# A two-layer fp32 trunk on one core: radix sums, cosine products, weights' low parts and gates from GpSimd to VectorE, and the second MLP's last folds spread

## The chip, the core and the metric

One core of a Trainium2 chip runs the whole program in one launch. The metric is the device time in microseconds (us), the median over several executions. PE is TensorE (matrix products), DVE is VectorE, ACT is ScalarE, POOL is GpSimd, SP is the engine whose queue issues most DMAs. All data are 32-bit floats.

## The reference

The program is a two-layer backbone over 1024 latent tokens and 256 context tokens of width 1024. Each layer has one input projection whose columns are split among differential attention (with an axial rope on q and k), a short gated convolution and a two-dimensional Fourier mix, then an output projection, a gated residual with a layer norm, and a squared-ReLU MLP with another gated residual and layer norm. Cut to what matters here:

```python
px = modulate(x, sh1, sc1) @ w_in[l]                  # input projection
qx, kx, vx, ux, gbx, gcx, fx = split_proj(px)
qx = axial_rope(qx, rows, cols)                       # x*cos + shuffled(x)*sin
kx = axial_rope(kx, rows, cols)
fourier_mix(fx)                                       # real part of an FFT over tokens and channels
...
x = layer_norm(ALPHA * x + g1 * mix_x, ln1_g[l], ln1_b[l])
x = layer_norm(ALPHA * x + g2 * squared_relu_mlp(modulate(x, sh2, sc2), w_up[l], w_down[l]),
               ln2_g[l], ln2_b[l])
```

## The kernel before

**Products.** Every fp32 product is made of three matmuls over high and low parts (`mm3`, L233 to L235): high by high, high by low, low by high. The high part is a rounding cast, mostly on ACT; the low part is `lo` (L229), one subtraction x - high. So each operand must pass through a cast and a subtraction before PE can use it, and the third matmul of a group is the first that needs the stationary operand's low part.

**Order.** The parts of the program that the change touches run under a manual schedule: every engine gets its instructions in the order in which the code is written, and runs them first in, first out. Generators interleave the work of the units by hand.

**The input projection** (`in_steps`) walks over 15 units per layer (two heads each of q and k pairs, v, u, c, g). A unit of layer 0 is 1280 columns wide and contracts over 1024, so it is 24 matmuls for each piece of 512, 512 and 256 columns. While a unit runs, `slot` advances four kinds of side work: `weights()` (L808 to L812), which converts the next unit's weights with `wconv` (ACT cast L2290, low part L229); `qk` (L556 on), the rope of the last q or k: drain on ACT (L561 or L563), shuffle on DVE (L566), cosine product (L567), sine product (L568), sum (L570), split (L581, L229) and store; `fourier1` (L638 on), the token transform's first radix step, some sixteen sums and differences (L645 to L664) of tiles of 128, 256 and 512 columns for each half of f, then a cast (L669) and a low part; and `fourier_mats` (L722 and L755 are its casts), small matmuls between the units. For layer 0, `PW` puts the low parts of the weights for units 4 to 12 on POOL; the others are on DVE. The first pass of the modulation (L336, L338, products with L383) for later stages is spread among the same slots on DVE.

**The first MLP's end** (`finish_steps`) handles ten tiles of 128 tokens. For each tile PE makes two halves of 24 matmuls in all, DVE adds each half to the running sum (L2378), POOL multiplies it by the gate (`gate`, L2382), DVE adds the residual (L2386), then come bn_stats (L2392), small statistics (L1265 to L1269 on DVE, L1270 and L1271 on POOL) and the norm on ACT (L2394). In `turn` the normed tiles are transposed (L2417) and modulated (L2426, L2429) for the next layer's input projection.

**The second MLP's end** (`finish_last`, with `fold`, `hl` and `rload` in the function before it) has eight tiles. During the last products, a table `tail` says after which product what is done: `hl` loads and splits the last rows of the hidden activations, `fold(t)` multiplies the running sum of tile t by the gate (L2171, POOL) and adds the residual (L2172, DVE). In `finish_last` the call `pre(t)` folds four tiles more; then, per tile, two halves are added on DVE (L2335), with bn_stats (L2336), statistics, norm (L2316, ACT), the product with the norm's weight (L2318, POOL), the sum with its bias (L2321, DVE) and the store. The last tile ends with L2346 and L2348 on DVE.

Of the kernel before, what the change touches and what calls it, by code (L numbers as in the profile page):

```python
# [13 lines left out]
ALU = mybir.AluOpType  # L14
# [5 lines left out]
SEQ = 1024  # L20
# [15 lines left out]
BKU = {1: 2, 2: 1, 3: 2, 4: 2, 5: 1, 6: 1, 7: 2}  # L36
ORDER = ["q0 k1 k2* q1* v0 u0 c0 g0 u1 c1 g1 q2 k3 q3 v1", "k0 q0 k1* q1* v0 u0 c0 g0 u1 c1 g1 k2 q2 k3 q3 v1"]
BGK = 2
PW = ((3, 13), (20, 0))
FME = 0  # L40
BGF = 2
FMD = 2
# [103 lines left out]
class Prog:  # L146
# [255 lines left out]
    def fold(self, l, which, lc, ch, vecs):  # L402
        nc = self.nc
        A = self.sm([128, 2, KT], bufs=4, tag="fold")
        B = self.sm([128, 2, KT], bufs=4, tag="fold")
        for v in vecs:
            nc.vector.tensor_tensor(A[:, v], self.lnc[:, lc, which], self.modc[:, l, ch + 1, v], op=ALU.mult)
            nc.vector.tensor_tensor(B[:, v], self.lnc[:, lc, which + 1], self.modc[:, l, ch + 1, v], op=ALU.mult)
            nc.vector.tensor_tensor(B[:, v], B[:, v], self.modc[:, l, ch, v], op=ALU.add)
        return A, B  # L410
# [145 lines left out]
    def qk(self, ps, n, h, key):  # L556
        nc = self.nc
        x = self.s5()
        for s, o in ps:
            if key == "q":  # L560
                nc.scalar.mul(x[:, s], o, SCALE)  # L561
            else:
                nc.scalar.copy(x[:, s], o)  # L563
        yield
        sh = self.s4()
        nc.vector.stream_shuffle(sh, x[:, :SEQ], [i ^ 16 for i in range(32)])  # L566
        nc.gpsimd.tensor_tensor(x[:, :SEQ], x[:, :SEQ], self.rc, op=ALU.mult)  # L567
        nc.vector.tensor_tensor(sh, sh, self.rs, op=ALU.mult)  # L568
        yield
        nc.vector.tensor_tensor(x[:, :SEQ], x[:, :SEQ], sh, op=ALU.add)  # L570
        yield from self.split_out(x, n)
        hi, lo = self.hl_out.pop(0)
        dh = self.dr([128, TOK])
        dl = self.dr([128, TOK])
        self.store(dh[:, :n], hi[:, :n])
        self.store(dl[:, :n], lo[:, :n])
        self.qkd[(key, h)] = (dh, dl)
# [59 lines left out]
    def fourier1(self, f, n):  # L637
        nc = self.nc  # L638
        nr = n // 128
        eo = self.s4(F32, [128, 2, 4, 128])  # L640
        e, o = eo[:, 0], eo[:, 1]
        fv = f.rearrange("p (a q) -> p a q", q=128)
        R = self.s5(F32, [128, 10, 128])
        g = nc.gpsimd
        g.tensor_tensor(e, fv[:, 0:4], fv[:, 4:8], op=ALU.add)  # L645
        g.tensor_tensor(o, fv[:, 0:4], fv[:, 4:8], op=ALU.subtract)
        t = self.s4(F32, [128, 4, 128])
        g.tensor_tensor(t[:, 0:2], e[:, 0:2], e[:, 2:4], op=ALU.add)
        g.tensor_tensor(R[:, 0], t[:, 0], t[:, 1], op=ALU.add)
        g.tensor_tensor(R[:, 1], t[:, 0], t[:, 1], op=ALU.subtract)  # L650
        g.tensor_tensor(R[:, 3], e[:, 0], e[:, 2], op=ALU.subtract)
        g.tensor_tensor(R[:, 6], e[:, 1], e[:, 3], op=ALU.subtract)
        yield
        g.tensor_tensor(t[:, 2], o[:, 1], o[:, 3], op=ALU.subtract)
        g.tensor_tensor(t[:, 3], o[:, 1], o[:, 3], op=ALU.add)
        g.tensor_scalar(t[:, 2:4], t[:, 2:4], math.sqrt(0.5), 0.0, op0=ALU.mult, op1=ALU.add)
        g.tensor_tensor(R[:, 2], o[:, 0], t[:, 2], op=ALU.add)
        g.tensor_tensor(R[:, 4], o[:, 0], t[:, 2], op=ALU.subtract)
        yield
        g.tensor_tensor(R[:, 5], o[:, 2], t[:, 3], op=ALU.add)  # L660
        g.tensor_tensor(R[:, 7], o[:, 2], t[:, 3], op=ALU.subtract)
        if n > SEQ:
            g.tensor_tensor(R[:, 8], fv[:, 8], fv[:, 9], op=ALU.add)
            g.tensor_tensor(R[:, 9], fv[:, 8], fv[:, 9], op=ALU.subtract)  # L664
        yield
        yield
        hi = self.s5(F32R, [128, 10, 128])
        lo = self.s5(F32R, [128, 10, 128])
        nc.scalar.copy(hi[:, :nr], R[:, :nr])  # L669
        yield  # L670
        self.lo(lo[:, :nr], R[:, :nr], hi[:, :nr])
        self.comps.append((hi, lo))
# [109 lines left out]
    def in_steps(self, X, l, PS):  # L782
        nc = self.nc
# [13 lines left out]
        nxt = [0]  # L797
# [9 lines left out]
        def weights():  # L807
            need = 2 if units[min(nxt[0], len(units) - 1)][0] == "v" else 1  # L808
            if self.wraw and len(self.wrdy) < need:
                self.wconv(nc.gpsimd if PW[l][0] < nxt[0] < PW[l][1] else None)  # L810
            if len(self.wraw) < 1:
                self.wload()  # L812

        def slot(k):
            for g in list(post):
                if next(g, 0) == 0:
                    post.remove(g)
            weights()
            if not fq:
                tail()  # L820
                for _ in range(k if nxt[0] > BGF else 1):
                    next(bg, None)
# [36 lines left out]
        for i, u in enumerate(units):  # L859
# [21 lines left out]
            if u[0] in "kq":  # L881
                g = self.qk([(slice(0, m), ps[:, :m])], m, b, u[0])
            elif u[0] == "u":
                z[b] = self.s5()
                nc.scalar.copy(z[b][:, :n], ps[:, :n])
                g = None
            elif u[0] == "c":
                g = self.conv_gc(ps, l, b, n, z.pop(b))
            else:
                g = self.conv_gb(ps, b, n)  # L890
# [1156 lines left out]
    def down_blocks(self, l, NG):  # L2047
        nc = self.nc
        n = SEQ if l else TOK
        T, HB, NB = n // 128, n // 2, D // 2  # L2050
        act, v, g = nc.scalar, nc.vector, nc.gpsimd
# [105 lines left out]
        bk = {"x": [self.p1() for _ in al], "y": [self.p1() for _ in range(8 - TH)]}  # L2157
        W, H, S, HR = [], [], [], []
        xr = {}
        self.acc = acc  # L2160
        gate = lambda t: self.gs[int(t >= 8)][:, :D]

        def rload(t):
            if t < T:
                xr[t] = self.s5()
                self.load(xr[t][:, :D], self.X2d[t])

        def fold(t):
            if t < T:
                y = acc[t]  # L2170
                g.tensor_tensor(y, y, gate(t), op=ALU.mult)  # L2171
                v.scalar_tensor_tensor(y, xr.pop(t)[:, :D], ALPHA, y, op0=ALU.mult, op1=ALU.add)  # L2172
                rload(t + 2)

# [43 lines left out]
        P = lambda fn, *a: (lambda: fn(*a))  # L2218
        if l:
            tail = [[gload], [P(wl, 0)], [P(wl, 1), wm], [P(wl, 2), wm], [P(wl, 3), wm],  # L2220
                    [wm, P(rload, 0), P(rload, 1)], [P(hl, 0), P(hl, 1)], [P(fold, 0), P(hl, 2), P(fold, 1)],
                    [P(hl, 3), P(fold, 2), P(fold, 3)]]
            tail = {N - 4 * (9 - a) + b: f for a, fs in enumerate(tail) for b, f in enumerate(fs)}
        else:
            tail = {-20: P(wl, 0), -18: P(wl, 1), -16: whi, -15: wlo, -14: P(wl, 2), -13: whi, -12: wlo,
                    -11: P(hraw, 0), -10: whi, -9: wlo, -8: hconv, -7: P(hraw, 1), -6: P(wl, 3), -5: hconv,
                    -4: [P(hraw, 2), P(hraw, 3)], -3: [gload, P(rload, 0)], -2: hconv, -1: whi}
            tail = {N + k: f for k, f in tail.items()}
# [36 lines left out]
        evac(0)  # L2265
        if l:
            self.lastW = W
            self.finish_last(l, H, lambda: None, bk["x"] + bk["y"], lambda t: fold(t + 4))
            yield
            return  # L2270
        wlo()
# [83 lines left out]
    def finish_steps(self, l):  # L2355
        nc = self.nc
        T = TOK // 128
        A, B = self.fold(l + 1, 2, l, 0, (0, 1))
        W, H = self.lastW, self.lastH
# [19 lines left out]

        def gate(t):  # L2380
            y = self.acc[t]
            nc.gpsimd.tensor_tensor(y, y, self.gs[int(t >= 8)], op=ALU.mult)  # L2382

        def resid(t):
            y = self.acc[t]
# [13 lines left out]
        def down(t):  # L2399
            if t < T:  # L2400
                half(t, 0)
            if t:
                resid(t - 1)
            if t < T:
                half(t, 512)
            if t:
                norm(t - 1)
            if t < T:
                gate(t)
                rload(t + 1)  # L2410
# [109 lines left out]
```

## Time and profile before

| | |
|---|---|
| time, median of 3 runs | 2889.89 us (2889.15 to 2890.15) |
| profiled execution's own time | 2883.89 us |
| its span in the trace | 2882.0 us |
| mean granted PE clock over the span | 0.979 |
| PE busy | 2714.8 us (94%), 14290 matmuls |
| DVE busy | 1990.0 us (69%), 2921 instructions |
| ACT busy | 1157.7 us (40%), 1614 instructions |
| POOL busy | 1092.1 us (38%), 660 instructions |

A number is read as follows. The span runs from the first to the last event of one execution; its own time is 1.9 us more. A row of a timeline gives start, duration, engine, source line and tiles, and in square brackets how long the engine sat idle before it and what released it. A row of groups gives a line's count, summed time, mean in ns, and idle time. Durations of neighbours on one engine overlap a little, so starts tell the pace.

### The profile page before, as it was taken

What the parts mean: (1) busy time and instruction counts of PE and PEld (TensorE: products, weight loads), DVE (VectorE), ACT (ScalarE), POOL (GpSimd) and SP (SyncE); (2) the same over time, 40 slices, a digit from 0 to 9 for tenths busy, and PEclk for the clock granted to TensorE, in tenths of its full rate; (3) what the DMA queues carried; (4) which work ended last, traced back from release to release, by engine and by line L of the source; (5) the groups of instructions that cost most, each with busy time, mean ns of one, the idle gap of its engine ahead of it and who ended that gap; (6) DMA issues with size and microseconds to landing.
All of it is one profiled execution on the core that took longest, in us unless ns stands there. A gap on an engine that the chain in (4) does not pass through costs nothing.

```text
span 2882.0 us, 37823 instructions
## 1 busy us (share of the span) xinstructions
PE 2714.8 (94%) x14290; PEld 2325.7 (81%) x14290; DVE 1990.0 (69%) x2921; ACT 1157.7 (40%) x1614; POOL 1092.1 (38%) x660
## 2 busy tenths in 40 slices
PE   7899999999999999899998999999999999999986
PEld 5788888778899999788886788888778778778865
DVE  6658767844578886677775555677645777668887
ACT  4221156623444444533332421266624545454331
POOL 2511145733110000276656600155763000078795
PEclk9999999999999999999999999999999999999998
DMA  7234553347546553634343244653356465554451
GB/s 269 86 144 155 168 144 89 120 139 254 217 176 221 184 191 137 236 129 152 135 163 122 90 161 155 200 123 90 121 187 211 158 234 198 179 204 159 153 185 59
DMA packets 228746, 468.17 MB, mean 162 GB/s; under 512 B 18926, under 2 KB 116692, under 8 KB 228564
## 3 DMA queue, kind: packets, MB, share of 16 engines
q1 hardware_dynamic: 208392, 394.39, 41.9%
q10 hardware_dynamic: 17292, 61.93, 5.6%
q0 software_dynamic: 2880, 9.44, 0.9%
q8 instruction: 113, 1.85, 0.3%
q14 instruction: 69, 0.57, 0.1%
HBM read 322.36 MB, written 143.31 MB: 162 GB/s over the span
## 4 chain that ended last, share of the span: by engine, by line
PE 51%; DVE 7%; POOL 4%; issue 4%; DMA 4%; ACT 3%; SPq 0%; ACTq 0%; DVEq 0%; POOLq 0%
PE q L233 13%; PE q L235 13%; PE q L234 13%; PE p L233 2%; PE p L235 2%; PE p L234 2%; PE q L1020 2%; POOL a L229 1%; PE p L955 1%; PE p L956 1%; DVE a L229 1%; PE q L1007 1%; DMA a<-d 1%; DMA b<-wu 1%; POOL b L2382 1%
## 5 line engine op out<-in xcount | busy, mean ns | idle before, releaser
L233 PE MATMUL q<-a,a 128*128 128x512 f32 (+1 forms) x1611 | 586.8, 364 | 34.2 <-DVE b L2237 15.2
L235 PE MATMUL q<-a,a 128*128 128x512 f32 (+2 forms) x1658 | 599.3, 361 | 5.0 <-DVE a L229 5.0
L234 PE MATMUL q<-a,a 128*128 128x512 f32 (+1 forms) x1594 | 580.2, 364 | 3.4 <-POOL a L229 3.4
L234 PE MATMUL p<-a,b 128*128 128x512 f32 (+1 forms) x1064 | 397.1, 373 | 1.1 <-POOL a L229 1.0
L233 PEld LDWEIGHTS q<-a,a 128*128 128x128 f32 x1611 | 304.2, 189 | 82.5 <-ACT a L2098 10.9
L229 POOL TENSOR_TENSOR a<-b,a 128x256 fp32r<-128x256 f32 (+1 forms) x137 | 220.7, 1618 | 349.9 <-ACT a L2098 196.5
L235 PEld LDWEIGHTS q<-a,a 128*128 128x128 f32 x1658 | 313.1, 189 | 47.7 <-DVE a L229 6.1
L2237 DVE TENSOR_TENSOR b<-q,b 128x512 f32<-128x512 f32 x405 | 268.4, 684 | 108.4 <-PE q L235 107.3
L234 PEld LDWEIGHTS q<-a,a 128*128 128x128 f32 x1594 | 301.4, 189 | 45.8 <-POOL a L229 4.5
L229 DVE TENSOR_TENSOR a<-a,a 128x1024 fp32r<-128x1024 f32 (+4 forms) x163 | 271.1, 1665 | 41.8 <-ACT a L2095 21.4
L233 PE MATMUL p<-a,b 128*128 128x512 f32 (+1 forms) x792 | 295.1, 373 | 1.5 <-ACT b L2290 1.0
L235 PE MATMUL p<-a,b 128*128 128x512 f32 (+1 forms) x776 | 283.3, 365 | 4.0 <-POOL b L229 2.4
L233 PE MATMUL q<-b,a 128*128 128x256 f32 (+1 forms) x748 | 256.0, 342 | 14.9 <-DVE b L2378 6.0
L234 PE MATMUL q<-b,a 128*128 128x256 f32 (+1 forms) x748 | 253.4, 339 | 0.7 <-DVE b L229 0.7
L235 PE MATMUL q<-b,a 128*128 128x256 f32 (+1 forms) x748 | 253.0, 338 | 0.0
L338 DVE SCALAR_TENSOR_TENSOR m<-w,k,m 128x256 f32<-128x256 f32 x448 | 219.6, 505 | 20.6 <-DMA w<-wmr 11.0
L234 PEld LDWEIGHTS p<-a,b 128*128 128x128 f32 x1064 | 202.8, 191 | 32.7 <-POOL a L229 1.9
L965 DVE TENSOR_REDUCE c<-p 128x1 f32<-128x1280 f32 x128 | 190.7, 1490 | 55.5 <-PE p L956 42.1
L981 ACT ACTIVATE a<-p,c 128x1280 f32<-128x1280 f32 x128 | 170.4, 1331 | 68.6 <-DVE c L965 50.1
L233 PEld LDWEIGHTS q<-b,a 128*128 128x128 f32 x748 | 144.0, 192 | 37.5 <-DVE b L2378 7.3
L233 PEld LDWEIGHTS p<-a,b 128*128 128x128 f32 x792 | 150.8, 190 | 25.6 <-issue 2.7
L235 PEld LDWEIGHTS p<-a,b 128*128 128x128 f32 x776 | 147.4, 190 | 29.4 <-POOL b L229 3.3
(297 smaller groups left out, 5398.5 us busy)
## 6 DMA issues: line engine op xcount, KB each, us to landing
a<-d SPq DMA_DIRECT2D x85, 512.0 KB
w<-wmr SPq DMA_DIRECT2D x160, 256.0 KB
a<-d SPq DMA_DIRECT2D x56, 640.0 KB
b<-wu SPq DMA_DIRECT2D x64, 512.0 KB
d<-t SPq DMA_DIRECT2D x46, 640.0 KB
b<-wd SPq DMA_DIRECT2D x52, 512.0 KB
d<-a ACTq DMA_DIRECT2D x40, 640.0 KB
a<-d SPq DMA_DIRECT2D x80, 320.0 KB
```

The source lines that it names most:

```text
L229: (eng or self.nc.vector).tensor_tensor(out, x, hi, op=ALU.subtract)
L233: mm(out, lh, rh, start=start, stop=False, skip_group_check=on)
L234: mm(out, lh, rl, start=False, stop=False, skip_group_check=on)
L235: mm(out, ll, rh, start=False, stop=stop, skip_group_check=on)
L338: nc.vector.scalar_tensor_tensor(a, w[:, i], s, a, op0=ALU.mult, op1=ALU.add)
L955: nc.tensor.matmul(ps[:, c:c + w], Q[p][:, qs], K[p][0][:, ks], start=True, stop=False)
L956: nc.tensor.matmul(ps[:, c:c + w], Q[p][:, qs], K[p][1][:, ks], start=False, stop=True)
L965: nc.vector.reduce_max(mx, ps[:, :nkey], axis=AX.X, negate=True)
L981: self.nc.scalar.activation(e[:, :nkey], ps[:, :nkey], AF.Exp, bias=mx, accum_out=s)
L1007: nc.tensor.transpose(pt[:, i], e, self.ident)
L1020: nc.tensor.matmul(po[:, :256], V[i // 8][:, i % 8], aT[i // 4][:, i % 4], start=i == 0, stop=i == 9)
L2237: v.tensor_tensor(a, ps, a, op=ALU.add)
```

## The change

Five edits. The cosine product of `qk` goes from POOL to DVE (16 instructions of 128x1024). The radix sums of `fourier1` go from POOL to DVE (four calls). `PW` is gone, so the low parts of the weights for units 4 to 12 of layer 0 are DVE's (10 of 128x1024). The gates of both MLPs' ends go from POOL to DVE (10 in `finish_steps`, 8 in `fold`). And the folds of the second MLP's end stand elsewhere: the table runs fold 0, `hl(2)`, fold 1, `hl(3)` after four products in turn, then fold 2; the other five folds are called from `finish_last` before tiles 0, 1, 2, 3 and 5 rather than before tiles 0 to 3 alone. What stays on POOL: the low parts of attention's and `turn`'s tiles, the gated weights `wm` (L2182), L2318, and the statistics L1270 and L1271. PE's order of instructions does not change.

```diff
-PW = ((3, 13), (20, 0))
@@ qk
-        nc.gpsimd.tensor_tensor(x[:, :SEQ], x[:, :SEQ], self.rc, op=ALU.mult)
+        nc.vector.tensor_tensor(x[:, :SEQ], x[:, :SEQ], self.rc, op=ALU.mult)
@@ fourier1
-        g = nc.gpsimd
+        g = nc.vector
@@ in_steps, weights()
-                self.wconv(nc.gpsimd if PW[l][0] < nxt[0] < PW[l][1] else None)
+                self.wconv()
@@ fold
-                g.tensor_tensor(y, y, gate(t), op=ALU.mult)
+                v.tensor_tensor(y, y, gate(t), op=ALU.mult)
@@ tail of the second MLP (l = 1)
-                    [wm, P(rload, 0), P(rload, 1)], [P(hl, 0), P(hl, 1)], [P(fold, 0), P(hl, 2), P(fold, 1)],
-                    [P(hl, 3), P(fold, 2), P(fold, 3)]]
+                    [wm, P(rload, 0), P(rload, 1)], [P(hl, 0), P(hl, 1)],
+                    [P(fold, 0), P(hl, 2), P(fold, 1), P(hl, 3)], [P(fold, 2)]]
@@
-            self.finish_last(l, H, lambda: None, bk["x"] + bk["y"], lambda t: fold(t + 4))
+            self.finish_last(l, H, lambda: None, bk["x"] + bk["y"], lambda t: fold({0: 3, 1: 4, 2: 5, 3: 6, 5: 7}.get(t, T)))
@@ finish_steps, gate
-            nc.gpsimd.tensor_tensor(y, y, self.gs[int(t >= 8)], op=ALU.mult)
+            nc.vector.tensor_tensor(y, y, self.gs[int(t >= 8)], op=ALU.mult)
```

One line less at the top makes every line number of the changed kernel one lower: the cosine product is L566 there, the radix sums are L644 to L663.

**DVE in layer 0's input projection, around the rope of k1 (tile a_904).** Here b_928 is the shuffled copy, b_595 the sine table and b_593 the cosine table, a_847 the second half's radix result, b_933 the low part of the weights that PE needs next, m_ the modulation's sums. Before:

```order
L338 SCALAR_TENSOR_TENSOR m_799<-w_767,k_77,m_799 128x256 x2
L229 TENSOR_TENSOR a_893<-a_754,a_892 128x1280
L566 STREAM_SHUFFLE b_928<-a_904 128x1024
L568 TENSOR_TENSOR b_928<-b_928,b_595 128x1024
L229 TENSOR_TENSOR b_933<-b_794,b_932 128x1024
L338 SCALAR_TENSOR_TENSOR m_798<-w_796,k_77,m_798 128x256 x2
L229 TENSOR_TENSOR b_927<-b_924,b_926 128x1024
L570 TENSOR_TENSOR a_904<-a_904,b_928 128x1024
```

and now:

```order
L228 TENSOR_TENSOR a_893<-a_754,a_892 128x1280
L659 TENSOR_TENSOR a_847<-b_846,b_850 128x128
L660 TENSOR_TENSOR a_847<-b_846,b_850 128x128
L662 TENSOR_TENSOR a_847<-a_728 128x128
L663 TENSOR_TENSOR a_847<-a_728 128x128
L565 STREAM_SHUFFLE b_928<-a_904 128x1024
L566 TENSOR_TENSOR a_904<-a_904,b_593 128x1024
L567 TENSOR_TENSOR b_928<-b_928,b_595 128x1024
L228 TENSOR_TENSOR b_933<-b_794,b_932 128x1024
L337 SCALAR_TENSOR_TENSOR m_798<-w_796,k_77,m_798 128x256 x2
L228 TENSOR_TENSOR b_927<-b_924,b_926 128x1024
L569 TENSOR_TENSOR a_904<-a_904,b_928 128x1024
```

The last four radix sums and the cosine product now stand in DVE's own queue, ahead of the weights' low part b_933, and the sum a_904 no longer depends on another engine.

**DVE at the first MLP's end, one tile.** b_10577 and b_10589 are the running sums of two neighbouring tiles, a_12934 the residual, c_ the statistics. Before:

```order
L2378 TENSOR_TENSOR b_10577<-q_12951,b_10577 128x512
L2392 BN_STATS c_12965<-b_10567 128x6 x2
L1265 BN_AGGR c_12968<-c_12965 128x2
L1267 TENSOR_SCALAR c_12970<-c_12968 128x1
L1269 TENSOR_SCALAR c_12972<-c_12968 128x1
L2378 TENSOR_TENSOR b_10589<-q_12982,b_10589 128x512
L2386 SCALAR_TENSOR_TENSOR b_10577<-a_12934,b_10577 128x1024
```

and now:

```order
L2377 TENSOR_TENSOR b_10577<-q_12951,b_10577 128x512
L2391 BN_STATS c_12965<-b_10567 128x6 x2
L1264 BN_AGGR c_12968<-c_12965 128x2
L1266 TENSOR_SCALAR c_12970<-c_12968 128x1
L1268 TENSOR_SCALAR c_12972<-c_12968 128x1
L2381 TENSOR_TENSOR b_10577<-b_10577,a_12857 128x1024
L2377 TENSOR_TENSOR b_10589<-q_12982,b_10589 128x512
L2385 SCALAR_TENSOR_TENSOR b_10577<-a_12934,b_10577 128x1024
```

The gate stands between the last small statistic of the tile before and the next tile's first half, one place ahead of the residual that needs it.

**DVE at the second MLP's end, where the last products end.** b_21290 to b_21332 are the running sums of tiles 3 to 7, a_22870 the gate, q_ the products. Before:

```order
L2172 SCALAR_TENSOR_TENSOR b_21281<-a_23183,b_21281 128x1024
L2237 TENSOR_TENSOR b_21300<-q_21238,b_21300 128x512
L2172 SCALAR_TENSOR_TENSOR b_21290<-a_23207,b_21290 128x1024
L2237 TENSOR_TENSOR b_21311<-q_21239,b_21311 128x512
L2237 TENSOR_TENSOR b_21323<-q_21240,b_21323 128x512
L2237 TENSOR_TENSOR b_21332<-q_21241,b_21332 128x512
L2172 SCALAR_TENSOR_TENSOR b_21300<-a_23238,b_21300 128x1024
L2335 TENSOR_TENSOR b_21258<-q_21238,b_21258 128x512
```

and now:

```order
L2236 TENSOR_TENSOR b_21332<-q_21241,b_21332 128x512
L2236 TENSOR_TENSOR b_21300<-q_21238,b_21300 128x512
L2236 TENSOR_TENSOR b_21311<-q_21239,b_21311 128x512
L2236 TENSOR_TENSOR b_21323<-q_21240,b_21323 128x512
L2236 TENSOR_TENSOR b_21332<-q_21241,b_21332 128x512
L2170 TENSOR_TENSOR b_21290<-b_21290,a_22870 128x1024
L2171 SCALAR_TENSOR_TENSOR b_21290<-a_23207,b_21290 128x1024
L2334 TENSOR_TENSOR b_21258<-q_21238,b_21258 128x512
```

No fold stands among the last four drains any more, and one fold of two instructions, gate and residual together, stands ahead of the first tile of `finish_last`.

## Rows read from the trace of the kernel before

**Rows 1.** The page's part 1: busy time of each engine.
```profile
PE 2714.8 (94%) x14290; PEld 2325.7 (81%) x14290; DVE 1990.0 (69%) x2921; ACT 1157.7 (40%) x1614; POOL 1092.1 (38%) x660
```

**Rows 2.** Windows, layer 0's input projection: length, PE, PEld, DVE, ACT, POOL busy; clock; DMA.
```profile
120.00:140.00 20.00, 9.29 (x50) 7.80 (x50) 16.19 (x19) 5.57 (x6) 7.98 (x6) 0.80 0.33 118
...
260.00:280.00 20.00, 20.00 (x110) 17.31 (x109) 19.54 (x35) 2.21 (x2) 3.16 (x1) 1.00 0.52 173
```

**Rows 3.** PE's timeline, same stage: three of its waits.
```profile
131.85 0.47 PE L233 MATMUL p<-b,b 128*128 128x128 f32 x1 [4.09 <-ACT b L722]
...
139.15 0.47 PE L235 MATMUL p<-b,b 128*128 128x128 f32 x1 [6.62 <-DVE b L229]
...
202.07 1.87 PE L383 MATMUL q<-m,k 128*2 128x256 f32 x4 [4.92 <-ACT b L604]
```

**Rows 4.** POOL's timeline, same stage: two cosine products.
```profile
122.21 2.39 POOL L567 TENSOR_TENSOR a<-a,b 128x1024 f32<-128x1024 f32 x1
...
134.04 3.38 POOL L567 TENSOR_TENSOR a<-a,b 128x1024 f32<-128x1024 f32 x1 [9.44 <-DVE b L566]
```

**Rows 5.** DVE's timeline, same stage.
```profile
124.64 1.23 DVE L570 TENSOR_TENSOR a<-a,b 128x1024 f32<-128x1024 f32 x1 [2.71 <-POOL a L567]
...
135.14 3.36 DVE L229 TENSOR_TENSOR b<-b,b 128x1024 fp32r<-128x1024 f32 x1
...
195.88 3.39 DVE L338 SCALAR_TENSOR_TENSOR m<-w,k,m 128x256 f32<-128x256 f32 x3
199.19 1.22 DVE L570 TENSOR_TENSOR a<-a,b 128x1024 f32<-128x1024 f32 x1
```

**Rows 6.** Groups of DVE instructions, whole span: tensor by tensor, 1024, 512 and 256 columns.
```profile
L568 DVE TENSOR_TENSOR b<-b,b 128x1024 f32<-128x1024 f32 x16 | 19.7, 1232 | 0.5
...
L1645 DVE TENSOR_TENSOR a<-b 128x512 f32<-128x512 f32 x14 | 9.5, 682 | 0.0
L1502 DVE TENSOR_TENSOR w<-w,m 128x256 f32<-128x256 f32 x72 | 30.1, 419 | 5.9 <-DMA w<-d 5.9
```

**Rows 7.** Groups of POOL instructions, 80 to 380 us.
```profile
L567 POOL TENSOR_TENSOR a<-a,b 128x1024 f32<-128x1024 f32 x8 | 26.1, 3268 | 101.2 <-DVE b L566 73.3 <-issue 15.2 <-DMA b<-d 12.7
```

**Rows 8.** PE's waits, 1530 to 1600 us: sum, times, longest.
```profile
PE q L233 <- DVE b L2378: 6.0, 4, 2.3
PE q L2417 <- DVE w L2426: 2.4, 1, 2.4
```

**Rows 9.** DVE's timeline at the first MLP's end, two residuals in turn.
```profile
1533.79 1.23 DVE L2386 SCALAR_TENSOR_TENSOR b<-a,b 128x1024 f32<-128x1024 f32 x1 [2.62 <-POOL b L2382]
...
1540.51 1.23 DVE L2386 SCALAR_TENSOR_TENSOR b<-a,b 128x1024 f32<-128x1024 f32 x1 [2.61 <-POOL b L2382]
...
1585.26 3.39 DVE L2386 SCALAR_TENSOR_TENSOR b<-b,b 128x1024 f32<-128x1024 f32 x1 [3.19 <-POOL b L2382]
```

**Rows 10.** PE's waits, layer 1's input projection, 1610 to 1875 us.
```profile
PE p L235 <- DVE b L229: 3.7, 2, 2.4
...
PE q L383 <- ACT b L604: 2.0, 1, 2.0
```

**Rows 11.** PE's waits, 2780 to 2882 us.
```profile
PE q L233 <- DVE b L2237: 12.0, 3, 7.3
```

**Rows 12.** DVE's timeline at the second MLP's end.
```profile
2815.33 1.21 DVE L2172 SCALAR_TENSOR_TENSOR b<-a,b 128x1024 f32<-128x1024 f32 x1
...
2827.11 3.40 DVE L2172 SCALAR_TENSOR_TENSOR b<-a,b 128x1024 f32<-128x1024 f32 x1 [3.23 <-POOL b L2171]
...
2874.50 1.23 DVE L2321 TENSOR_TENSOR b<-b,b 128x1024 f32<-128x1024 f32 x1 [2.44 <-POOL b L2318]
```

**Rows 13.** POOL's timeline there.
```profile
2827.05 2.38 POOL L2318 TENSOR_TENSOR b<-b,b 128x1024 f32<-128x1024 f32 x1
```

**Rows 14.** Windows of the end, columns as in rows 2.
```profile
2820.00:2840.00 20.00, 20.00 (x90) 16.57 (x89) 12.71 (x17) 2.49 (x2) 10.87 (x8) 1.00 0.00 1
...
2860.00:2880.00 20.00, 0.00 (x0) 0.00 (x0) 15.92 (x29) 3.72 (x3) 11.45 (x12) 0.56 0.32 126
```

## The prediction

> **What bounds the kernel now.** I read the page's busy times first: PE is busy for 2714.8 of 2882.0 us [rows 1], so the work moved here is not what the time is made of, and a gain can only come out of PE's idle time, some 167 us, and out of its clock. So the next views were PE's waits by stage, and the windows. Three stages that the change touches show waits that end at the moved work or just behind it, and the end of the program is a fourth.
>
> In layer 0's input projection PE waits three times for long: 4.09 us for the cast L722, 6.62 us for a low part on DVE, and 4.92 us for the drain L604 [rows 3]. In the window 120 to 140 it is busy for 9.29 of 20 us and the granted clock is 0.80 [rows 2]. POOL finishes the radix sums only at 122.21, runs the cosine product next [rows 4], DVE waits for that 2.71 us before it can add (L570) [rows 5], and ACT's next casts stand behind that sum.
>
> In the first MLP's end PE waits 6.0 us in four pieces for DVE's drains, and 2.4 us once more for a transposed tile [rows 8]. DVE's rows say why: from one residual to the next it is 6.72 us (1533.79 to 1540.51), and 2.61 us of that is a wait for POOL's gate [rows 9]. PE's own pace there is 24 matmuls a tile; at 20.00 us for 90 matmuls of that size [rows 14] that is 5.33 us. So DVE, with an idle hole, is the slower of the two.
>
> At the second MLP's end PE has 12.0 us of waits for DVE's drains [rows 11], and the program does not end with PE: in the window 2860 to 2880 PE shows 0.00, DVE 15.92 [rows 14].
>
> **The prices.** A tensor by tensor instruction of 128x1024 costs DVE 1232 ns where nothing disturbs it, 682 ns at 512 columns, 419 ns at 256 [rows 6]; the same slope gives some 0.29 us at 128 (an estimate). POOL takes 3268 ns for a cosine product [rows 7]. So one call of the radix sums (two of 512, one of 256, twelve of 128 and a scaling near 0.35) is 5.6 us on DVE; on POOL the two calls of layer 0 hold the next cosine product back until 122.21 [rows 4].
>
> DVE is not only replacing; it is also disturbed now. A residual takes 1.21 us at 2815.33 and 3.40 us at 2827.11, where POOL's L2318 runs from 2827.05 for 2.38 us [rows 12, 13]: the second waits inside itself until POOL is done. The low part at 135.14 takes 3.36 us beside the cosine product of 134.04 [rows 4, 5]. Taking such instructions off POOL therefore also shortens DVE's other rows.
>
> **Layer 0's input projection.** I added the new rows to DVE's queue in the order shown, with these prices and the casts' times. The weights' low part b_933, which PE waits for there, comes 0.4 us later by this count, since the radix sums now stand ahead of it. The sum L570 at 124.64 moves 3.6 us up, with it two casts and two stores on ACT, the next drain, and L722: the wait of 4.09 shrinks to about 0.4. The low part that ends the 6.62 us wait comes near 134.3 rather than 139.15, because the shuffle starts 2.5 us sooner and the 3.36 us row is 1.23: -4.8 us, with a wait of some 5.6 us left. I take nothing back for the clock. At 199.19 the sum L570 [rows 5] gets free of a product on POOL and of stretched rows: +1.15 for the cosine, +1.15 for a low part, less 2.0 of stretching in the row at 195.88 (three sums of some 0.47 in 3.39) and 2.1 in the row ahead of it, makes 1.8 us sooner, and the 4.92 shrinks to 3.1. At the last rope, before v1, 1.1 us. A low part ahead of the Fourier matmuls' one near 166 costs 0.7. Sum: -4.8 - 1.8 - 1.1 + 0.7 = **-7.0 us**. Ends: -2 (the 128-column sums cost as much as the 256 ones, 0.42: 24 x 0.13 = 3.1 us later at L570) to -9.5 (the clock of the window 120 to 140 comes back in part).
>
> The low parts of the units between cost nothing by my count: each is 1.23 us on DVE per unit of 24 x 2.5 matmuls of 0.22 = 13.3 us; the cover is a whole unit of lead. In the fullest window DVE is busy 19.54 of 20 [rows 2] though, and if that cover goes, this is the price of the second rival.
>
> **The first MLP's end.** The cycle of DVE becomes 6.72 - 2.61 + 1.15 = 5.26 us (starts stand some 0.08 closer than durations), just under PE's 5.33. Then drains no longer hold PE: of the 6.0 us I keep 1.0 for the first tile. At the last tile a wait of 3.19 and a residual of 3.39 [rows 9] become two instructions of 1.23, 4.1 us less ahead of the transposes, and the wait of 2.4 for L2426 [rows 8] goes. Sum -5.0 - 2.4 = **-7.4 us**; ends -4 (the two paces are so near that half the waits stay) to -11.
>
> **Layer 1's input projection.** Same parts, smaller waits: 3.7 us in two for DVE's low parts, of which I take 3.5, and 1.0 of the 2.0 for L604 [rows 10]. **-4.5 us**; ends -2 to -6.5.
>
> **The second MLP's end.** The first of the 12.0 us of waits, 7.3 us [rows 11], lies ahead of the folds and stays. Of the other 4.7 I take 2.7, because the drains no longer queue behind a residual that waits for POOL's gate; bounds 0.5 and 4. Behind the first tile of `finish_last` three folds now have a wait like the 3.23 and a residual like the 3.40 [rows 12]: 6.63 us each, 19.9 in all. Instead four folds of two instructions stand there (before tiles 1, 2, 3 and 5), 2.46 us each if nothing disturbs them and 4.84 if each runs into one L2318 of 2.38 [rows 13]: 9.8 to 19.4 us. So DVE gets 0.5 to 10 us back. I take 4.0, nearer to the lower end, since the L2318 at 2827.05 came just when a fold stood there, and since PE's 192 matmuls (43 us) and the last tile's chain through POOL (the 2.44 us wait at 2874.50) do not get shorter. Sum -2.7 - 4.0 = **-6.7 us**; ends -1 to -12.
>
> **The sum.** -7.0 - 7.4 - 4.5 - 6.7 = -25.6 us on the profiled execution's 2883.89, so 2858.3. The median of the runs is 6.0 above that execution, so the time is **2864.3 us**, 0.9% less. A difference under 0.2%, 5.8 us, could not be told from none here.
>
> **Rivals.** *The waits move on (chance 0.20).* PE's waits are shortened where they are, but the next release is late too: in the first MLP's end the paces 5.26 and 5.33 are equal within the reading, in the input projections the 5.6 us wait still lets the clock fall, at the end L2318 meets the folds. Half of the 7.4, the 7.0 and the 4.5, nothing at the end: -9.5, so 2880. For it: DVE takes on work in stages where it is 60 to 80% busy. Against: POOL's gate is what DVE waits for, in every tile [rows 9].
>
> *DVE falls behind in layer 0's units (chance 0.07), the slower end.* Between 160 and 365 us DVE gets eight low parts and three cosine products more. If they come after a bunch of modulation sums that already fill a window [rows 2], the unit's first third matmul waits. At 3.4 us, the length of the stretched rows, for each of nine units, it is 30.6 us, and the stage's own 7.0 is lost; less the other stages' 18.6, it is +12.0: 2902. It decides from the point at which DVE is more than a unit's 13.3 us behind. Against it: PE shows no wait at all there now, and the fullest window still leaves DVE 0.46 us.
>
> *The two engines only take turns (chance 0.06).* A DVE instruction which meets one on POOL stands until POOL's is done [rows 5, 12, 13]. Where that is so everywhere, what POOL loses DVE pays, and PE's waits stay where they are: 2890, give or take 4, against 2864 by the sum. Against it: the wait for the gate is 2.61 us [rows 9], a gate on DVE 1.23, and the radix sums shrink from POOL's pace to DVE's. The Trainium skill ("Perfetto Trace Analysis", section "Optimizing Scalar/DVE Operations") has this case as a rule: GpSimd and DVE share an SBUF read port, so that moving operations between the two might not help, and a saturated DVE should rather be relieved. That the two get in each other's way, the trace agrees; that the sum of both is fixed, it does not.
>
> *The stretching was the larger part (chance 0.12).* If DVE's rows beside POOL shrink everywhere as the stretched ones would [rows 5, 12], and the clock of 120 to 160 comes back, every term is at its far end: -9.5 - 11 - 6.5 - 10 = -37: 2853. Against it: PE still has a wait of over 5 us there, and its order is unchanged.
>
> The forecast itself (2857 to 2873) has 0.55.
>
> **Numbers.** Range 2850 to 2883: it takes in the far ends and the first rival. Faster by more than 0.2%: 0.83; within: 0.10; slower by more than 0.2%: 0.07.
>
> **What will show it.** Right: in the profile after, no wait for POOL before L2385 and PE's waits for L2377 nearly gone; a third matmul near 134 in place of 139.15; the residuals at the end near 1.23, or stretched where L2317 runs. Wrong: PE waits for weights' low parts between 160 and 365 us; DVE's tile cycle over 5.5 us in the first MLP's end; or the last drain still some 63 us after the start of the last matmuls.

## The result, and the profile after

The changed kernel takes 2863.92 us (median of 3 runs, 2858.97 to 2864.28) against 2889.89; the ratio is 0.9898, 95% interval 0.9884 to 0.9913. 2864.3 was forecast. Its profiled execution took 2863.92 us too, with a span of 2861.8, so the two profiled executions differ by 20.0 us and the medians by 26.0: the profiled execution of before lies 6.0 under its median. Line numbers of the changed kernel are one lower.

The page's part 1 after, beside [rows 1]:

```profile
PE 2722.8 (95%) x14290; PEld 2334.9 (82%) x14290; DVE 2001.1 (70%) x3025; ACT 1157.9 (40%) x1614; POOL 940.6 (33%) x556
```

POOL gave up 104 instructions and 151.5 us; DVE took the 104 and grew by 11.1 us only. By their durations after, the 104 take some 77 us there, so DVE's other instructions got shorter by most of what it took on.

PE's timeline after, layer 0's input projection, beside [rows 3]:

```profile
119.42 0.50 PE L234 MATMUL p<-a,b 128*128 128x512 f32 x1 [1.95 <-DVE b L228]
...
134.85 0.47 PE L234 MATMUL p<-b,b 128*128 128x128 f32 x1 [5.86 <-DVE b L228]
...
196.01 1.02 PE L382 MATMUL q<-m,k 128*2 128x256 f32 x4 [3.06 <-ACT b L603]
```

The 4.09 us wait is gone, the third matmul starts at 134.85 (134.3 was forecast), the 4.92 is 3.06 (3.1 forecast).

At the first MLP's end: PE's waits after between 1530 and 1600 us, beside [rows 8], then DVE's timeline, beside [rows 9], then ACT's.

```profile
PE q L232 <- DVE b L2377: 4.0, 2, 3.3
PE p L232 <- ACT b L2289: 3.8, 1, 3.8
PE p L234 <- POOL b L228: 2.3, 1, 2.3
```

```profile
1521.16 1.22 DVE L2385 SCALAR_TENSOR_TENSOR b<-a,b 128x1024 f32<-128x1024 f32 x1
...
1524.87 1.21 DVE L2381 TENSOR_TENSOR b<-b,a 128x1024 f32<-128x1024 f32 x1
...
1526.60 1.21 DVE L2385 SCALAR_TENSOR_TENSOR b<-a,b 128x1024 f32<-128x1024 f32 x1
1528.01 0.69 DVE L2377 TENSOR_TENSOR b<-q,b 128x512 f32<-128x512 f32 x1 [0.20 <-PE q L234]
```

```profile
1571.48 1.24 ACT L2393 ACTIVATE b<-b,c,c 128x1024 f32<-128x1024 f32 x1 [4.99 <-POOL c L1270]
...
1573.12 1.04 ACT L2289 CAST b<-b 128x1024 fp32r<-128x1024 f32 x1 [0.40 <-ACT b L2393]
```

DVE's cycle is 5.44 us instead of 6.72 and no longer has the hole for POOL; it is DVE that waits now, 0.20 us a tile for PE. But in the tiles behind, PE still waits 4.0 us for drains, and it now waits 3.8 us for the cast L2289 of the next weights, which is queued on ACT behind a norm that sat for 4.99 us. The window 1570 to 1590, columns as in [rows 2], has the clock at 0.74:

```profile
1570.00:1590.00 20.00, 13.95 (x57) 10.43 (x57) 8.68 (x16) 10.18 (x13) 11.99 (x11) 0.74 0.44 151
```

At the second MLP's end, DVE's timeline after, beside [rows 12], then POOL's, beside [rows 13], then the window, beside [rows 14]:

```profile
2809.06 0.69 DVE L2334 TENSOR_TENSOR b<-q,b 128x512 f32<-128x512 f32 x1 [1.67 <-PE q L234]
...
2812.21 1.22 DVE L2170 TENSOR_TENSOR b<-b,a 128x1024 f32<-128x1024 f32 x1
2813.45 1.23 DVE L2171 SCALAR_TENSOR_TENSOR b<-a,b 128x1024 f32<-128x1024 f32 x1
...
2817.74 1.83 DVE L2170 TENSOR_TENSOR b<-b,a 128x1024 f32<-128x1024 f32 x1
...
2822.08 1.21 DVE L2320 TENSOR_TENSOR b<-b,b 128x1024 f32<-128x1024 f32 x1
...
2825.03 1.61 DVE L2170 TENSOR_TENSOR b<-b,a 128x1024 f32<-128x1024 f32 x1
2826.67 1.23 DVE L2171 SCALAR_TENSOR_TENSOR b<-a,b 128x1024 f32<-128x1024 f32 x1
...
2836.36 1.86 DVE L2170 TENSOR_TENSOR b<-b,a 128x1024 f32<-128x1024 f32 x1
...
2854.26 1.23 DVE L2320 TENSOR_TENSOR b<-b,b 128x1024 f32<-128x1024 f32 x1 [2.44 <-POOL b L2317]
```

```profile
2822.24 3.31 POOL L2317 TENSOR_TENSOR b<-b,b 128x1024 f32<-128x1024 f32 x1 [1.36 <-ACT b L2315]
...
2825.51 1.53 POOL L1269 TENSOR_TENSOR c<-c,k 128x1 f32<-128x1 f32 x1
```

```profile
2820.00:2840.00 20.00, 20.00 (x90) 16.57 (x89) 19.52 (x30) 4.18 (x4) 15.16 (x10) 1.00 0.20 79
```

DVE is busy for 19.52 of 20 us (12.71 before) and, behind the 1.67 us for PE at 2809.06, has no wait until the last tile. Residuals take 1.23 us. POOL's L2317 and L1269 are stretched now, and three of the four gates behind the first tile take 1.61 to 1.86 us. The first drain of `finish_last`, at 2809.06 here, stood before at

```profile
2820.65 0.69 DVE L2335 TENSOR_TENSOR b<-q,b 128x512 f32<-128x512 f32 x1 [0.58 <-PE q L235]
```

**Where the 20 us came from.** PE runs the same matmuls in the same order, so the start of the n-th matmul in two timelines gives the head start at that point. Each column is its change over one stage, against the trace of before, in us (minus: time won). In that trace the first five stages end at 380, 1510, 1610, 1875 and 2780 us; "last" runs to the end of the span. No edit lies in the columns "attention 0" and "attention 1" (each with the MLP's products behind it).

```
                          proj. 0  attention 0  MLP 1 end  proj. 1  attention 1  last    sum
the change                  -8.6       +4.3        -3.2      -4.4       +2.0    -10.4   -20.2
the same, second profile   -10.3       +3.4        -3.2      -4.6       +2.5     -9.0   -21.2
s2 projections back         -0.7       +0.4        -3.3      +3.0       +3.1     -9.6    -7.1
s3 gate one back            -9.2       +1.4        -0.1      -4.4       +1.7    -10.1   -20.6
s4 end back                 -9.3       +0.3        -3.6      -5.4       +4.6     +0.9   -12.4
s5 radix back              -15.1       +2.0        -3.7      -5.0       +1.3     -9.0   -29.5
s6 cosine back              -2.6       +5.1        -3.7      +4.1       +0.8    -11.1    -7.5
s7 lows back               -10.7       +2.1        -2.9      -4.3       +2.3    -10.1   -23.6
s8 casts before norm        -9.6       -0.1        -5.6      -5.3       +1.5    -10.3   -29.4
s9 radix back, casts       -10.5       +1.7        -5.6      -4.5       +1.3    -11.1   -28.8
s10 and lows back          -14.0       +3.7        -5.7      -4.7       +5.1     -9.7   -25.4
s11 end gate back          -10.1       -1.1        -3.6      -5.5       +5.1     +7.0    -8.2
s12 end folds back          -9.6       +3.7        -3.1      -4.3       +2.1    -11.8   -23.0
```

Where an edited stage has the same code, its step agrees within some 2 us from run to run, except in s9, whose first column lies 4.6 above that of s5. The stages without an edit range from -1.1 to +5.1.

### The profile page after: what moved, and what is told of

Read it like the earlier page. It is cut to its first block, busy times and chain, and to the rows that moved or that the text cites. A ratio compares the mean times of both kernels' runs of the same rounds, so it can differ in the third digit from the quotient of the medians.

```text
span 2861.8 us, 37789 instructions
## 1 busy us (share of the span) xinstructions
PE 2722.8 (95%) x14290; PEld 2334.9 (82%) x14290; DVE 2001.1 (70%) x3025; ACT 1157.9 (40%) x1614; POOL 940.6 (33%) x556
## 3 DMA queue, kind: packets, MB, share of 16 engines
q0 software_dynamic: 2880, 9.44, 0.9%
## 4 chain that ended last, share of the span: by engine, by line
PE 53%; DVE 7%; issue 4%; DMA 4%; POOL 3%; ACT 3%; SPq 0%; ACTq 0%; DVEq 0%; POOLq 0%
PE q L232 14%; PE q L234 13%; PE q L233 13%; PE p L232 2%; PE p L234 2%; PE p L233 2%; PE q L1019 2%; DVE a L228 1%; PE p L954 1%; PE p L955 1%; DMA a<-d 1%; POOL a L228 1%; PE q L1006 1%; POOL b L2317 1%; DVE b L2236 0%
## 5 line engine op out<-in xcount | busy, mean ns | idle before, releaser
L995 POOL TENSOR_SCALAR a<-a,c 128x768 f32<-128x768 f32 x64 | 87.5, 1367 | 696.3 <-DVE c L990 664.5
L228 DVE TENSOR_TENSOR a<-a,a 128x1024 fp32r<-128x1024 f32 (+4 forms) x163 | 264.3, 1623 | 42.3 <-ACT a L2094 21.0
L232 PE MATMUL q<-b,a 128*128 128x256 f32 (+1 forms) x748 | 255.5, 342 | 11.1 <-DVE b L2377 4.0
L337 DVE SCALAR_TENSOR_TENSOR m<-w,k,m 128x256 f32<-128x256 f32 x448 | 209.7, 483 | 20.7 <-DMA w<-wmr 11.0
```

Source lines behind the costliest of these rows:

```text
L228: (eng or self.nc.vector).tensor_tensor(out, x, hi, op=ALU.subtract)
L232: mm(out, lh, rh, start=start, stop=False, skip_group_check=on)
L337: nc.vector.scalar_tensor_tensor(a, w[:, i], s, a, op0=ALU.mult, op1=ALU.add)
L995: nc.gpsimd.tensor_scalar(E[1][:, r], E[1][:, r], cf, 0.0, op0=ALU.mult, op1=ALU.add)
```

## The experiments

Each kernel is the changed one with the edit shown, and is compared with the kernel before on the same chip. A ratio's interval is about 0.0014 to either side; two ratios that differ by under 0.0020 (0.0014 times the root of 2), or 5.8 us, are not told apart.

**s1, the change again.** 

> The changed kernel as it is, to size its gain in more rounds. The profiled executions differ by 20.0 us and the medians by 26.0. Theory A (the profiles are typical, the 6 us between the profile of before and its median are chance): about 20 us faster, ratio 0.993. Theory B (the medians are typical): 26 us, ratio 0.991.

Measured: 2862.63 us, ratio 0.9903 (0.9890 to 0.9917), 28 us under the kernel before. The medians were typical, theory B. The profile of before is a lucky execution: its 2883.89 lies under every run of before on record (2885.16 to 2895.45). So the table, which counts from it, shows some 6 us less than was won, and in which stage those lie is not known.

**s2, the projections' edits undone.** cosine products and radix sums to `nc.gpsimd`, and

```diff
-                self.wconv()
+                self.wconv(nc.gpsimd if ((3, 13), (20, 0))[l][0] < nxt[0] < ((3, 13), (20, 0))[l][1] else None)
```

> The changed kernel with the three edits of the input projections undone (cosine products, radix sums and weights' low parts of units 4 to 12 on POOL again). Theory A (the gain is in PE's waits there, as the two traces' equal matmuls show: 9.5 us earlier after layer 0's projection, 4.3 more after layer 1's, some 6 given back in the stages behind): it loses 8 to 14 us against the change. Theory B (the prediction's terms): it loses 11.5. Rival (the stages that follow absorb any head start, since PE's clock falls at other places): it loses under 4.

Measured: 2879.18 us, ratio 0.9961 (0.9949 to 0.9974): it loses 0.0058, or 16.8 us, above theories A (8 to 14) and B (11.5), though the noise takes in all from 11.0 on; the rival is excluded. By the table layer 0's projection loses 7.9 to 9.6 and layer 1's some 7.5; in the latter the head start from the first MLP's end (-3.3) is given back as well (+3.0). There the granted clock is lower for nearly the same work. A window of before, then of s2:

```profile
1680.00:1700.00 20.00, 18.71 (x136) 17.44 (x135) 11.23 (x9) 7.92 (x9) 2.23 (x1) 1.00 0.43 159
```

```profile
1680.00:1700.00 20.00, 18.68 (x127) 17.43 (x126) 9.79 (x11) 7.82 (x8) 0.15 (x1) 0.91 0.42 159
```

**s3, the first MLP's gate on POOL.**

```diff
-            nc.vector.tensor_tensor(y, y, self.gs[int(t >= 8)], op=ALU.mult)
+            nc.gpsimd.tensor_tensor(y, y, self.gs[int(t >= 8)], op=ALU.mult)
```

> The changed kernel with the gate of the first MLP's end on POOL again. Theory A (the trace after shows a head start of 4.2 us made there and 2.0 lost again before the next stage, behind a cast of weights that waits for the norm on ACT's queue): it loses 2 to 3 us. Theory B (the prediction's term): it loses 7.4. Rival (the stage is bound by something else): 0.

Measured: 2862.89 us, ratio 0.9902 (0.9887 to 0.9917): no difference from the change that can be told. The stage itself shows -0.1 against -3.2, so the edit is worth some 3.1 us there, near theory A and too little for the whole time to show. The forecast's 7.4 is excluded.

**s4, the end as before.**

```diff
-                v.tensor_tensor(y, y, gate(t), op=ALU.mult)
+                g.tensor_tensor(y, y, gate(t), op=ALU.mult)
...
-                    [P(fold, 0), P(hl, 2), P(fold, 1), P(hl, 3)], [P(fold, 2)]]
+                    [P(fold, 0), P(hl, 2), P(fold, 1)], [P(hl, 3), P(fold, 2), P(fold, 3)]]
...
-lambda t: fold({0: 3, 1: 4, 2: 5, 3: 6, 5: 7}.get(t, T))
+lambda t: fold(t + 4)
```

> The changed kernel with the second MLP's end as before: gate on POOL, folds in their old places. Theory A (the head start grows from 10.3 to 20.2 us there): it loses 10 us. Theory B (the prediction's term): 6.7. Rival (DVE and POOL take turns, nothing gained): 0.

Measured: 2871.53 us, ratio 0.9934 (0.9922 to 0.9947): it loses 0.0031, or 9.0 us. The rival is excluded; theories A and B are not told apart by the time.

**s5, the radix sums alone on POOL.**

```diff
-        g = nc.vector
+        g = nc.gpsimd
```

> The changed kernel with the radix sums alone on POOL again (both layers). All three projection edits together were worth 16.6 us. Theory A (the radix sums hold the chain radix, cosine, L570, casts on ACT, low part at the start of both projections): this alone loses most, 8 to 14 us. Theory B (the cosine product is what POOL is late with): under 4. Rival C (the parts replace each other: with the radix sums back the cosine product on DVE still frees the chain): about 0.

Measured: 2856.35 us, ratio 0.9877 (0.9863 to 0.9890): none of the three. It is 0.0026, or 7.5 us, faster than the change, with intervals that just touch; s9 below does not repeat that gain. POOL's timeline of before, then of s5:

```profile
90.27 3.38 POOL L567 TENSOR_TENSOR a<-a,b 128x1024 f32<-128x1024 f32 x1 [15.16 <-issue]
93.61 1.28 POOL L645 TENSOR_TENSOR b<-a 128x512 f32<-128x512 f32 x1
```

```profile
81.23 1.29 POOL L644 TENSOR_TENSOR b<-a 128x512 f32<-128x512 f32 x1 [5.82 <-ACT a L849]
...
104.19 1.20 POOL L663 TENSOR_TENSOR a<-a 128x128 f32<-128x128 f32 x1
```

Before, POOL sat idle for 15.16 us with the cosine product at the head of its queue, until DVE's shuffle (88.80 to 90.14) was through; the radix sums stood behind it. Without that product in the queue they start 12.4 us sooner and end at 105.39 instead of 122.24, on the slow engine. PE's wait at 119.42 is gone and the long one is 4.31 (PE's timeline of s5):

```profile
130.72 0.33 PE L234 MATMUL p<-b,b 128*128 128x128 f32 x1 [4.31 <-DVE b L228]
```

So moving the radix sums to DVE was not needed, and in layer 0 it delays a weights' low part (118.15 after, 113.96 in s5). In layer 1's projection the step is the same with either.

**s6, the cosine products alone on POOL.**

```diff
-        nc.vector.tensor_tensor(x[:, :SEQ], x[:, :SEQ], self.rc, op=ALU.mult)
+        nc.gpsimd.tensor_tensor(x[:, :SEQ], x[:, :SEQ], self.rc, op=ALU.mult)
```

> The changed kernel with the cosine products alone on POOL again. With the radix sums gone from POOL's queue the cosine product starts at once and costs 2.4 to 3.4 us in place of 1.2, and it stretches DVE's rows beside it, 16 times, of which some five end at a wait of PE. Theory A: it loses 3 to 6 us. Theory B (it is the product that PE waits for, not the radix sums): 8 or more. Rival C: 0.

Measured: 2876.68 us, ratio 0.9952 (0.9940 to 0.9965): it loses 14.2 us, theory B. The cosine product is nearly the whole worth of the projections' edits. No radix sum stands behind it in POOL's queue here, so holding those up can't be what it costs. POOL's, DVE's and PE's timelines of s6, then its waits from 110 to 225 us:

```profile
116.83 3.38 POOL L566 TENSOR_TENSOR a<-a,b 128x1024 f32<-128x1024 f32 x1 [22.70 <-DVE b L565]
```

```profile
117.93 3.36 DVE L228 TENSOR_TENSOR b<-b,b 128x1024 fp32r<-128x1024 f32 x1
```

```profile
121.35 0.80 PE L234 MATMUL p<-a,b 128*128 128x512 f32 x1 [3.83 <-DVE b L228]
```

```profile
PE p L234 <- DVE b L228: 11.3, 3, 5.6
PE q L382 <- ACT b L603: 3.7, 1, 3.7
```

Beside POOL's product the weights' low part b_933 takes 3.36 us, and PE waits 3.83 us for it; in the change it takes 1.22 (at 118.15) and the wait is 1.95. The two kinds of wait are 3.3 us more than in the change (8.6 and 3.1 there), and the granted clock is 0.78 and 0.88 between 120 and 160 us, against 0.83 and 1.00.

**s7, the weights' low parts alone on POOL** (the diff of s2). 

> The changed kernel with the low parts of the weights for units 4 to 12 on POOL again. The trace of before shows no wait of PE between 222 and 362 us, so theory A expects no loss, within 2 us either way. Theory B (POOL's low parts stretch DVE's modulation sums and rope by up to 2.3 us each, ten of them, and some stand ahead of a wait): it loses 3 to 5. Rival C (DVE is the fuller engine there): it gains 1 to 3.

Measured: 2860.93 us, ratio 0.9892 (0.9879 to 0.9906): no difference that can be told. Theory B's loss is excluded; theory A and rival C are not told apart.

**s8, the casts ahead of the norm.** In `down(t)` of `finish_steps`, between the second half and the norm:

```diff
+            if t in (8, 9):
+                self.wconv(nc.gpsimd)
+            if t == 8:
+                self.wload()
             if t:
                 norm(t - 1)
...
-            if t == 8:
-                self.wconv(nc.gpsimd)
-                self.wload()
-        self.wconv(nc.gpsimd)
         down(T)
```

> The changed kernel with one thing moved at the first MLP's end: the casts of the next layer's first two weight tiles (L2289) are issued on ACT ahead of the norm of the tile before, not behind it. In the trace after, PE waits 3.8 us for the first cast, which stands behind a norm that waits for POOL's statistics, and 2.3 us more for its low part, and its granted clock in the 20 us behind that is 0.74. Theory A (the gate's gain was lost to this queue): 4 to 8 us faster than the change, and both waits nearly gone. Theory B (the weights' load is what is late): 0. Rival C (the norms come later and the transposes wait): slower by 1 to 3.

Measured: 2856.22 us, ratio 0.9879 (0.9863 to 0.9894): 0.0024, or 6.9 us, under the change; the intervals overlap a little, and theory A fits. The stage's step is -5.6 in this run, and -5.6 and -5.7 in the two below, against -3.2. ACT's timeline of s8, and the window, where the change had 0.74:

```profile
1561.04 1.06 ACT L2289 CAST b<-b 128x1024 fp32r<-128x1024 f32 x1
...
1568.93 1.24 ACT L2393 ACTIVATE b<-b,c,c 128x1024 f32<-128x1024 f32 x1 [6.83 <-POOL c L1270]
```

```profile
1570.00:1590.00 20.00, 17.00 (x89) 13.46 (x90) 5.08 (x11) 11.45 (x16) 13.80 (x13) 1.00 0.17 61
```

The first cast is done 12 us sooner (some 5 of them are the head start of the stages ahead) and PE's wait for it is gone, but 3.5 us of waits for POOL's low parts stay.

**s9, radix sums on POOL and casts first** (the diffs of s5 and s8). 

> The changed kernel with the radix sums back on POOL and the two casts ahead of the norms. Theory A (the two gains lie in different stages and add: 6.3 and 6.4 us): some 2850 us, 12 to 13 us under the change and 40 under the kernel before. Rival (one head start is given back in the stage behind, as some always is): 2854 to 2856.

Measured: 2856.10 us, ratio 0.9883 (0.9869 to 0.9896): the rival. The table says where the sum fell short: layer 0's projection gave -10.5 with the very code that gave -15.1 in s5. Against s8 (0.9879) the radix sums on POOL win nothing that can be told. The windows of s5 and of s9 there:

```profile
180.00:200.00 20.00, 16.93 (x135) 15.83 (x134) 17.28 (x29) 4.19 (x8) 0.00 (x0) 1.00 0.53 197
```

```profile
180.00:200.00 20.00, 16.69 (x112) 14.82 (x110) 18.25 (x29) 4.66 (x9) 0.00 (x0) 0.83 0.44 159
```

The same code, with the granted clock at 1.00 and at 0.83: 135 matmuls and 112.

**s10, the weights' low parts on POOL as well.** 

> As the run before, with the weights' low parts of units 4 to 12 on POOL too, so that of the projections' edits only the cosine product is left on DVE. Theory A (POOL was late in the projections only because the cosine product stood at the head of its queue and waited there for DVE's shuffle; what stays on POOL costs nothing): within 2 us of the run before. Rival (POOL's low parts stretch DVE's rows at the projections' waits): 3 to 5 us slower. Rival (DVE is relieved): 2 to 3 faster.

Measured: 2852.05 us, ratio 0.9874 (0.9859 to 0.9888), not to be told from the run before: no loss of 3 to 5 us shows, and theory A and the rival of 2 to 3 us faster are not told apart. Nor is it slower than s8 (0.9879), which has all three edits of the projections: the cosine product alone carries their gain. This is the lowest median of the study, though not told apart from s5, s8 and s9; its interval lies under that of s1 (0.9890 to 0.9917) and meets that of the first measurement (0.9884 to 0.9913).

**s11, only the second gate on POOL** (first hunk of s4). 

> The changed kernel with only the second MLP's gate on POOL again, the folds spread as in the change. The whole edit of the end is worth 8.9 us. Theory A (the wait for POOL's gate and the residual that meets POOL's next product are what went): it loses 6 to 9. Theory B (the places of the folds are what matters): it loses 1 to 3.

Measured: 2878.19 us, ratio 0.9966 (0.9954 to 0.9979): it loses 18.2 us, twice what was expected and more than the whole edit undone (s4, 0.9934). DVE's waits of s11, 2790 to 2880 us:

```profile
DVE b L2171 <- POOL b L2170: 15.3, 6, 3.5
DVE b L2334 <- PE q L234: 3.0, 1, 3.0
```

The waits for POOL's gate are nearly the same in s4 (14.5 us in 7). But there three folds come behind the first tile of `finish_last`, and here four, each with such a wait and a stretched residual, 6.9 us together. DVE's timeline of s11, the fourth:

```profile
2849.22 3.35 DVE L2171 SCALAR_TENSOR_TENSOR b<-a,b 128x1024 f32<-128x1024 f32 x1 [3.52 <-POOL b L2170]
```

**s12, only the folds in their old places** (the other hunks of s4). 

> The changed kernel with only the folds in their old places, the gate on DVE. Theory A (the gate's engine is the gain): it loses 0 to 3. Theory B (the places): it loses 6 to 8. Both edits needed together: both this run and the one before lose 5 or more.

Measured: 2859.58 us, ratio 0.9896 (0.9883 to 0.9910): no loss that can be told, theory A. With the gate on DVE the places of the folds make no difference that shows; with the gate on POOL the new places cost 9 us more (s11 against s4).

## Why the prediction was right, and where it was not

The time came out within 0.4 us, closer than its terms deserve. By the profiles two terms were too small (layer 0's projection and the second MLP's end), one was over twice too large (the first MLP's end), and some 6 us given back in the stages without an edit were in no term. That these cancel is luck. Against the medians the sum of 25.6 us was right (26.0, and 28.4 in s1); against the lucky profile of before it was too large (20.2 and 21.2).

- **Layer 0's projection, -7.0.** The steps in two profiles are -8.6 and -10.3. Each wait came out as worked: 134.85 for 134.3, 3.06 for 3.1; the low part b_933 cost 0.4 more wait (1.95 for 1.53). What failed is what held the chain: "on POOL the two calls of layer 0 hold the next cosine product back until 122.21 [rows 4]". True, but the calls themselves were late because a cosine product stood ahead of them, idle at the head of POOL's queue (s5's row of before, 15.16 us). Radix sums on DVE bring nothing (s9 and s10 against s8; s5 is even faster without them), the cosine product nearly everything (s6, s10). It costs in two ways on POOL: it holds back what stands behind it (before), and it stretches a low part that PE waits for (s6). The second the prediction had, with its price.
- **Layer 1's projection, -4.5.** The steps are -4.4 and -4.6. Its worth is more than that, though: with the cosine products on POOL the same stage has +3.0 and +4.1 (s2, s6). That the stage's own step was then positive, not zero, was not foreseen. The granted clock, 0.91 in the window 1680 to 1700 of both runs and 1.00 before, goes with it; why it falls there was not tried.
- **The first MLP's end, -7.4.** The step that failed: "of the 6.0 us I keep 1.0 for the first tile". The tile cycle was nearly right (5.44 for 5.26, with DVE waiting for PE). But 4.0 us of waits for drains stay in the tiles of the transposes, where DVE's L2425 stands ahead of them, and the head start meets the cast L2289 behind a norm on ACT: 3.8 us of new wait, and the clock at 0.74. It measured -3.2 in both profiles; s8 (-5.6) shows that the order on ACT's queue held back over 2 us of it.
- **The second MLP's end, -6.7.** Measured -10.4 and -9.0 in the profiles, 9.0 by s4. The term that was mis-sized is "I take 4.0, nearer to the lower end, since the L2318 at 2827.05 came just when a fold stood there". From the first drain of `finish_last` to the end of the span it is 61.4 us before (from 2820.65) and 52.7 after (from 2809.06), which is 8.6 less. A fold meets POOL's product, if at all, only in the product's last part: the four folds behind the first tile take 11.2 us from start to next start, near the forecast's lower bound of 9.8, where the three of before took 19.9. POOL's L2317 is stretched to 3.31 us beside DVE's L2320 (2822.08), not beside a fold, and DVE does not wait for it there. The other part, 2.7 for the drains, gave only 1.7 and 0.3.
- **The rivals.** DVE did not fall behind in layer 0's units: PE has no wait for a low part between 225 and 380 us, and putting them back changes nothing that can be told (s7). The prediction's "PE shows no wait at all there now" overlooked the 4.92 us at 202.07 of its own [rows 3]. The first rival, waits that move on, came true at the first MLP's end alone. The rule of the Trainium skill ("Perfetto Trace Analysis", "Optimizing Scalar/DVE Operations"), that moving work between GpSimd and DVE might not help, holds for the radix sums and the low parts (s9, s7) and not for the cosine products and the second gate (s6, s11). In these runs the moves that paid are those where work that PE or the last chain waits for stood behind the moved instruction or beside it; that this tells them apart elsewhere is not shown.

## What to carry to other kernels

In a kernel with in-order queues, look at what stands behind an instruction that waits at the head of a queue before pricing the instruction itself: a 3 us product that waited 15 us made the 29 us behind it some 12 us late, and moving it alone was enough. Look also at what runs beside it on the other engine: the same product made a low part of 1.22 us last 3.36. After a gain in one engine's cycle, the next thing in the other queues (here a cast behind a norm) decides how much of it arrives. And test the parts of a change one by one: three parts were worth 16.8 us together, of which one carried 14.2 and the other two nothing that can be told.

## What the runs showed of the hardware

POOL loses to DVE as DVE loses to POOL. L1270 of the kernel before, a POOL product of 128x1, is L1269 after, and stands there beside DVE's gate (1524.87 to 1526.08). POOL's timeline before, then after:

```profile
1530.59 0.55 POOL L1270 TENSOR_TENSOR c<-c,k 128x1 f32<-128x1 f32 x1 [3.57 <-DVE c L1269]
```

```profile
1524.97 1.52 POOL L1269 TENSOR_TENSOR c<-c,k 128x1 f32<-128x1 f32 x1 [2.54 <-DVE c L1268]
```

An instruction of one column per partition thus waits out a gate of 1024. And layer 0's projection took 4.6 us longer in s9 than in s5, though the two kernels have the same code up to there and PE's waits are nearly the same; the granted clock differs (0.83 and 1.00 from 180 to 200 us). Gains of that size can't be read from one profile.
